# 32 of the 384 dense tokens leave the first expert product; 48 gathers, 52 parked blocks and the gate reads are moved

## The chip, the cores and the metric

The kernel runs on one core of one Trainium2 chip. The core has a matrix engine (TensorE, PE in the profile, with its weight loads as PEld), a vector engine (DVE), a scalar engine (ACT), GpSimd (POOL, which here issues the indirect DMAs), SyncE (SP, which issues the plain DMAs) and 16 DMA engines. The metric is the device time of one execution in microseconds; a run's time is a little longer than the span from its first to its last instruction.

## The reference, cut to what matters

Two layers over 512 tokens of width 1024. Each layer has a mixer (attention in the first, a short convolution in the second) and then a PEER block, and each of the four starts with an RMS norm. The PEER block scores 128 x 128 experts per token through two sets of 128 keys, keeps 16 of them for each of 8 heads (128 per token), and sums the chosen experts' rows:

```
q  = (xc @ w_query) ...                       # per head and half
sv, si = top_k(q . keys, 16)                  # for both halves
cand = sv[0][:, None] + sv[1][None, :]        # 256 candidates
best, pos = top_k(cand, 16); eidx = 128 * i + j
g = softmax(best)
a   = einsum('cd,chkd->chk', xc, w_up[eidx])  # up: one dot product per chosen expert
act = gelu(a) * g
out = einsum('chk,chkd->cd', act, w_down[eidx])
```

Inputs and output are float32; w_up and w_down have 16384 rows of 1024 floats (4 KB) per layer.

## The kernel before, in words

Tokens are in four chunks of 128. In a PEER block the last chunk (c3) is handled **sparsely**: for each of its 128 expert slots, one indirect DMA on POOL's queue fetches 128 rows of w_up (one for each token, 512 KB), and DVE multiplies them with the normed tokens `hn` and sums (L477); later the same for w_down, multiplied by the activation and added to `accg` (L486). These are 256 gathers per layer, through a ring of 4 row buffers.

The other three chunks (TD = 384 tokens) are handled **densely**, for all 16384 experts, in 128 blocks of 128 experts. For each block an *up* (`dense_up`, matmuls at L127) loads 512 KB of transposed w_up, splits it into a high and a low part (ACT L105, DVE L106), and runs 24 matmuls of 128 x 128 by 384 columns (8 pieces of 3 products: high-high, high-low, low-high); ACT applies Gelu to the result `ab` (L499). A *down* (`dense_down`) multiplies `ab` by the gate matrix on DVE (`w`, L520), splits `w`, loads and splits 512 KB of w_down, and runs 18 matmuls of 512 columns into six accumulators that stay in PSUM (L536). Each tensor is kept as a high and a low float32r part.

The gate matrix (weight of each expert for each dense token) is built on the chip in the **retrieval** stage: DVE picks the top 16 (`select`, in the order of chunks 3, 0, 1, 2); then for each four tokens (a *quad*, 96 per layer) DVE and ACT build two sets of one-hot vectors `ob` and `oa`, PE multiplies them (L457), and ACT copies the result to `stage` (L458), which goes to DRAM as `gd` in 12 pieces of 2 MB. While DVE and ACT do this, PE runs ups: the first NPRE = 52 blocks are computed there, and their `ab` is written to DRAM (`ad`): these blocks are *parked*. How many up pieces go between two steps is set by estimated costs: each step yields an estimate for DVE and PE, and pieces (0.49 each) follow while the sum for PE is below PRE_RATE = 1.4 times the sum for DVE.

Then comes the **dense stage**: 128 downs, with the 76 fresh ups between them (AHEAD = 4 blocks ahead) and the 256 gathers spread over the blocks (a parked block counts 1, a fresh one 2; LATE = 0.97 ends them a little early). The gate matrix is read back in groups of 4 blocks (`gt`, 768 KB, two buffers), a parked `ab` in pairs (`at`). Groups of fresh and of parked blocks alternate so that both kinds are used up together. SP, POOL, DVE, ACT and PE each run their instructions in a fixed order, which a planner chose by simulating the program's timeline; `issue_after` ties a gather to its block's `w`.

Each norm (`norm_t`) computes a factor per token, writes it into a diagonal matrix `dg` (L168), and transposes and scales the tokens in one float32 product of `h` with `dg` (L174), 32 products per norm; each shows as two instructions. The gains and the split into high and low follow at L178 and L179.

Of the kernel before, what the change touches and what calls it, by code (L numbers as in the profile page):

```python
# [12 lines left out]
F32 = mybir.dt.float32  # L13
# [10 lines left out]
P = 128  # L24
# [26 lines left out]
NPRE = 52  # L51
PRE_RATE = 1.4
OB = 12
ACTN = 2
# [10 lines left out]
def encoder(ctx: ExitStack, tc: tile.TileContext, x, g_mix, g_ffn, g_ffn_row, g_fin_row, bias,  # L65
# [93 lines left out]
    def norm_t(gain, name, order=range(NCH)):  # L159


        xh = acts.tile([P, KC, S], F32R, name=f"xh{name}", tag="xh")
        xl = acts.tile([P, KC, S], F32R, name=f"xl{name}", tag="xl")
        dg = {}
        for c in order:
            r = rstd_of(c)
            dg[c] = small.tile([P, P], F32, name="dg", bufs=4)
            nc.vector.tensor_scalar(dg[c], ident, r, None, op0=ALU.mult)  # L168
        for k0 in range(0, KC, 4):
            ps = [ps_acc(f"ps_t{k}") for k in range(4)]  # L170
# [5 lines left out]
            for k in range(4):  # L176
                kc = k0 + k
                nc.scalar.activation(xh[:, kc], ps[k], AF.Copy, scale=gain[:, kc:kc + 1])  # L178
                nc.vector.scalar_tensor_tensor(xl[:, kc], ps[k], gain[:, kc:kc + 1], xh[:, kc].bitcast(F32),  # L179
                                               op0=ALU.mult, op1=ALU.subtract)  # L180
        return xh, xl
# [22 lines left out]
    def attention(l):  # L204
        xh, xl = norm_t(gm[:, l], f"m{l}", (3, 0, 1, 2) if l else range(NCH))
# [137 lines left out]
    def short_conv(l):  # L343
        xh, xl = norm_t(gm[:, l], f"m{l}", (3, 0, 1, 2) if l else range(NCH))
# [29 lines left out]
    ad = dram.tile([NPRE // 2, P, 2, TD], F32, name="ad")  # L374

    def peer(l):
        xh, xl = norm_t(gf[:, l], f"f{l}")
        with ExitStack() as st:
# [6 lines left out]
            r3 = rstd_of(c3)  # L385
            nc.vector.scalar_tensor_tensor(hn, h[:, c3], r3, hn, op0=ALU.mult, op1=ALU.mult)
# [24 lines left out]
            g3 = pp.tile([P, P], F32, name="g3")  # L411

            pr = p2

            def retrieval():

                for c in (3, 0, 1, 2):
                    it = select(sv[:, c], si[:, c], pr, cand)
                    while True:
                        try:  # L420
                            yield next(it), 0.0
                        except StopIteration as e:
                            gg, ii, jj = e.value
                            break
                    if c == c3:
                        nc.vector.scalar_tensor_tensor(eid, ii, float(NK), jj, op0=ALU.mult, op1=ALU.add)
                        if l:
                            nc.vector.tensor_scalar(eid, eid, float(l * NK * NK), None, op0=ALU.add)
                        nc.vector.tensor_copy(eidx, eid)
                        nc.vector.tensor_copy(g3, gg)  # L430
                    else:
                        ps = ps_acc("ps_g")
                        for n, t in enumerate((gg, ii, jj)):
                            nc.tensor.transpose(ps[:, n * P:(n + 1) * P], t, ident)
                        for n, t in enumerate((gT, iT, jT)):
                            nc.vector.tensor_copy(t[:, c * P:(c + 1) * P], ps[:, n * P:(n + 1) * P])
# [27 lines left out]
            ab = {}  # L464
            ag = pp.tile([P, P], F32, name="ag")
# [8 lines left out]
            def gather_up(k, t):  # L474
                fetch(up, k, t)
                o = acts.tile([P, D], BF16, name="sq", tag="sq")
                nc.vector.scalar_tensor_tensor(o, t, 1.0, hn, op0=ALU.mult, op1=ALU.mult,  # L477
                                               accum_out=ag[:, k:k + 1])
                if k % 4 == 3:
                    s = ag[:, k - 3:k + 1]  # L480
                    nc.scalar.activation(s, s, AF.Gelu)
                    nc.vector.tensor_tensor(s, s, g3[:, k - 3:k + 1], op=ALU.mult)

            def gather_down(k, t):
                fetch(down, k, t)
                nc.vector.scalar_tensor_tensor(accg, t, ag[:, k:k + 1], accg, op0=ALU.mult, op1=ALU.add)  # L486
# [7 lines left out]

            def dense_up(b):
                for ps in up_pieces(up_t[l, b], xh, xl, TD):
                    yield
                a = pp.tile([P, TD], F32, name="ab", tag="ab", bufs=AHEAD + 2)
# [9 lines left out]
            def dense_down(n, b):  # L508
                if b % 4 == 0:
                    gt = p2.tile([P, TD // GT, 4, GT], F32, name="gt")  # L510
                    nc.sync.dma_start(gt.rearrange("p g i c -> p g (i c)"),
                                      gd[:, :, b:b + 4].rearrange("g j i c -> j g (i c)"))
                    first.append(gt)
                if b < NPRE and b % 2 == 0:
                    at = p2.tile([P, 2, TD], F32, name="at")
                    nc.sync.dma_start(at, ad[b // 2])
                    ab[b], ab[b + 1] = at[:, 0], at[:, 1]
# [3 lines left out]
                                        ab.pop(b).rearrange("p (g c) -> p g c", c=GT), gt[:, :, b % 4], op=ALU.mult)  # L521
# [34 lines left out]

            fresh = list(range(NPRE // 4, NK // 4))
            kept = list(range(NPRE // 4))
            order = []
            for n, q in enumerate(fresh):  # L560
                order.append(q)
                while len(kept) and (NPRE // 4 - len(kept)) * len(fresh) <= n * (NPRE // 4):
                    order.append(kept.pop(0))
            order += kept
            blocks = [4 * q + i for q in order for i in range(4)]
            ng = done = 0
            rows = [p2.tile([P, D], F32, name=f"row{n}", bufs=1) for n in range(RING)]
            nup = NPRE
            for n, b in enumerate(blocks):
# [7 lines left out]
                while ng < len(gathers) and ng * (2 * NK - NPRE) * LATE < done * len(gathers):  # L577
                    fn, k = gathers[ng]
                    with tc.issue_after(mark):
                        fn(k, rows[ng % RING])  # L580
# [168 lines left out]
```

## Time and profile before

| | |
|---|---|
| median of 3 runs | 3028.08 us (3024.51 to 3029.07) |
| profiled execution, its own time | 3023.92 us |
| its span, first to last instruction | 3022.1 us |
| granted TensorE clock, mean | 0.997 |
| PE busy | 2985.9 us (99%) |
| DVE busy | 2337.9 us (77%) |
| ACT busy | 1362.3 us (45%) |
| POOL busy | 658.6 us (22%) |
| DMA moved | 747.96 MB, mean 247 GB/s |

Busy times are of each engine alone; they overlap. A PE that is busy need not be at its best pace, since matmuls are pipelined: the pace is read from the length of a run of matmuls in the chain of waits. The retrieval stages lie at about 400 to 715 us and 1850 to 2170 us, the dense stages at about 730 to 1555 us and 2185 to 3010 us.

### The profile page before, as it was taken

To read this page: it belongs to the slowest core of one execution; us is meant where nothing else is said; L and a number is where in the kernel's file an instruction comes from. 1 tells how busy PE (TensorE), PEld (TensorE's weight loads), DVE (VectorE), ACT (ScalarE), POOL (GpSimd) and SP (SyncE) were. 2 spreads that over 40 slices of the span, in tenths; PEclk is the share of its full clock that TensorE was granted. 3 is DMA by queue.
4 is the path that set the end of the run, shared out by engine and by line. 5 is a ranking of instruction groups with operands and counts; after the bars stand their busy time and mean duration, and the time that the engine had idled before them with its cause. 6 is when DMAs were issued, how large, how long until landed. Compare 5 with 4: busy or idle time off the path is not lost. (4 is left out here: it accounts for less than half of the span.)

```text
span 3022.1 us, 44124 instructions
## 1 busy us (share of the span) xinstructions
PE 2985.9 (99%) x15730; PEld 2677.1 (89%) x15730; DVE 2337.9 (77%) x5115; ACT 1362.3 (45%) x2237; POOL 658.6 (22%) x571
## 2 busy tenths in 40 slices
PE   8999999999999999999999999999999999999998
PEld 7887899999888888888888888999988888888887
DVE  4444899887888888887874489998788888888786
ACT  5444246996333333333342233599733333333333
POOL 0000000001434443443310000000034344444341
PEclk9999999999999999999999999999999999999999
DMA  4222244567999999998942323556699999999995
GB/s 162 95 97 89 87 138 159 220 233 282 340 344 340 337 344 338 333 338 316 340 144 92 108 93 114 171 196 232 239 358 340 334 348 335 340 326 350 324 332 192
DMA packets 297981, 747.96 MB, mean 247 GB/s; under 512 B 23456, under 2 KB 139168, under 8 KB 294688
## 3 DMA queue, kind: packets, MB, share of 16 engines
q1 hardware_dynamic: 224032, 476.67, 45.2%
q0 software_dynamic: 73728, 268.47, 24.0%
q8 instruction: 124, 2.03, 0.3%
q14 instruction: 97, 0.79, 0.1%
HBM read 672.17 MB, written 72.88 MB: 247 GB/s over the span
## 5 line engine op out<-in xcount | busy, mean ns | idle before, releaser
L127 PE MATMUL ps_up<-xhf,wu_l 128*128 128x384 f32 (+1 forms) x2304 | 798.9, 347 | 1.2 <-DVE wu_l L106 1.0
L127 PE MATMUL ps_up<-xhf,wu_h 128*128 128x384 f32 (+1 forms) x2304 | 794.2, 345 | 2.0 <-ACT ab L499 2.0
L127 PE MATMUL ps_up<-xlf,wu_h 128*128 128x384 f32 (+1 forms) x2304 | 792.0, 344 | 0.0
L105 ACT ACTIVATE wu_h<-wu_raw 128x1024 fp32r<-128x1024 f32 x336 | 355.4, 1058 | 710.6 <-PE ps_up L127 430.7
L470 POOL DMA_INDIRECT row<-in_up,eidx x256 | 322.4, 1260 | 1312.9 <-DMA wu_raw<-in_up_t 881.6
L536 PE MATMUL acc<-wd_h,w_l 128*128 128x512 f32 x1536 | 603.7, 393 | 0.1
L536 PE MATMUL acc<-wd_l,w_h 128*128 128x512 f32 x1536 | 599.0, 390 | 0.0
L105 ACT ACTIVATE wd_h<-wd_raw 128x1024 fp32r<-128x1024 f32 x256 | 271.6, 1061 | 702.0 <-issue 619.3
L106 DVE TENSOR_TENSOR wu_l<-wu_raw,wu_h 128x1024 fp32r<-128x1024 f32 x336 | 410.0, 1220 | 176.4 <-ACT wu_h L105 176.1
L536 PE MATMUL acc<-wd_h,w_h 128*128 128x512 f32 x1536 | 514.9, 392 | 0.0
L106 DVE TENSOR_TENSOR wd_l<-wd_raw,wd_h 128x1024 fp32r<-128x1024 f32 x256 | 313.3, 1224 | 235.5 <-ACT wd_h L105 234.9
L127 PEld LDWEIGHTS ps_up<-xhf,wu_h 128*128 128x128 f32 x2304 | 433.3, 188 | 21.1 <-ACT ab L499 3.3
L127 PEld LDWEIGHTS ps_up<-xlf,wu_h 128*128 128x128 f32 x2304 | 433.1, 188 | 17.5
L127 PEld LDWEIGHTS ps_up<-xhf,wu_l 128*128 128x128 f32 x2304 | 433.1, 188 | 17.2 <-DVE wu_l L106 3.7
L470 POOL DMA_INDIRECT row<-in_down,eidx x256 | 330.4, 1291 | 511.7 <-DVE sq L477 464.6
L536 PEld LDWEIGHTS acc<-wd_l,w_h 128*128 128x128 f32 x1536 | 288.4, 188 | 61.7
L486 DVE SCALAR_TENSOR_TENSOR accg<-row,ag,accg 128x1024 f32<-128x1024 f32 x256 | 327.4, 1279 | 16.1 <-DMA row<-in_down,eidx 15.5
L536 PEld LDWEIGHTS acc<-wd_h,w_l 128*128 128x128 f32 x1536 | 288.6, 188 | 55.0 <-DVE w_l L106 0.9
L536 PEld LDWEIGHTS acc<-wd_h,w_h 128*128 128x128 f32 x1536 | 287.2, 188 | 54.8
L477 DVE SCALAR_TENSOR_TENSOR sq<-row,hn 128x1024 bf16<-128x1024 f32 x256 | 312.0, 1219 | 3.9 <-DMA row<-in_up,eidx 2.7
L457 PE MATMUL ps_gb<-ob,oa 128*128 128x128 f32 x1536 | 209.6, 274 | 0.0
L458 ACT ACTIVATE stage<-ps_gb 128x512 f32<-128x512 f32 x192 | 204.6, 1114 | 2.1 <-PE ps_gb L457 1.5
(164 smaller groups left out, 3325.8 us busy)
## 6 DMA issues: line engine op xcount, KB each, us to landing
wd_raw<-in_down SPq DMA_DIRECT2D x256, 512.0 KB, 5.8
wu_raw<-in_up_t SPq DMA_DIRECT2D x256, 512.0 KB, 4.9
gd<-stage SPq DMA_DIRECT2D x24, 2048.0 KB, 7.4
gt<-gd SPq DMA_DIRECT2D x64, 768.0 KB, 9.2
ad<-ab SPq DMA_DIRECT2D x104, 192.0 KB, 2.1
at<-ad SPq DMA_DIRECT2D x52, 384.0 KB, 8.0
wu_raw<-in_w_query SPq DMA_DIRECT2D x32, 512.0 KB, 3.5
wu_raw<-in_w_qkv SPq DMA_DIRECT2D x24, 512.0 KB, 3.5
```

The costliest lines, as they stand in the source:

```text
L105: nc.scalar.activation(hi, raw, AF.Copy)
L106: nc.vector.tensor_tensor(lo, raw, hi.bitcast(F32), op=ALU.subtract)
L127: nc.tensor.matmul(ps[:, :n], a[:, c], b[:, kc, :n], start=k == 0, stop=k == 3 * KC - 1)
L457: nc.tensor.matmul(ps[:, n * NK:(n + 1) * NK], a, b4[:, n], start=True, stop=True)
L458: nc.scalar.activation(stage[:, :, 4 * q:4 * q + 4].rearrange("p i t -> p t i"), ps.rearrange("p (t i) -> p t i", t=4), AF.Copy)
L470: nc.gpsimd.indirect_dma_start(out=t, out_offset=None, in_=table, in_offset=bass.IndirectOffsetOnAxis(ap=eidx[:, k:k + 1], axis=0))
L477: nc.vector.scalar_tensor_tensor(o, t, 1.0, hn, op0=ALU.mult, op1=ALU.mult, accum_out=ag[:, k:k + 1])
L486: nc.vector.scalar_tensor_tensor(accg, t, ag[:, k:k + 1], accg, op0=ALU.mult, op1=ALU.add)
L536: nc.tensor.matmul(acc[c, half], aa[:, cs], ww[:, hs], start=new and i == 0, stop=n == NK - 1 and ww is held[-1][-1])
```

## The change

The last 32 tokens of the third chunk (tokens 352 to 383, a *unit*, UN = 1, UT = 32) no longer take part in the ups: an up has TU = 352 columns. Their up products come from gathers: the 128 partitions hold 32 tokens x 4 groups of slots, so 32 indirect DMAs fetch all 32 x 128 rows, and 32 DVE products with `hu` (the normed tokens, copied to all four groups) give the dots; Gelu, the gate weights and a transpose bring them into `gT`, so that the gate matrix holds activation times weight for these tokens. In `ab` and `at` their columns are set to 1.0 once, and downs are as before, for 384 tokens. The chunks are selected in the order 2, 3, 0, 1. After the unit's 32 gathers the first 48 of the sparse gathers follow, in the retrieval stage too, one step after each `select` step or quad. 104 blocks are parked instead of 52, the gate matrix is read in groups of 8 blocks (1.5 MB), and PRE_RATE is 1.56. In the norms, DVE scales the tokens (`hs`, 1024 columns per chunk) and PE transposes them against the identity; the factors are reused in the PEER block instead of computed again for chunk 3.

```diff
-NPRE = 52
-PRE_RATE = 1.4
+NPRE = 104
+UN = 1
+UT = 32
+TU = TD - UN * UT
+GB = 8
+PRE_RATE = 1.56
+EARLY = 48
 def norm_t(gain, name, order=range(NCH)):
-            dg[c] = small.tile([P, P], F32, name="dg", bufs=4)
-            nc.vector.tensor_scalar(dg[c], ident, r, None, op0=ALU.mult)
+                hs[c] = sp.tile([P, D], F32, name=f"hs{c}")
+                nc.vector.tensor_scalar(hs[c], h[:, c], r, None, op0=ALU.mult)
...
-                    nc.tensor.matmul(ps[k][:, c * P:(c + 1) * P], h[:, c, kc * P:(kc + 1) * P], dg[c],
-                                     start=True, stop=True)
+                        nc.tensor.transpose(ps[k][:, c * P:(c + 1) * P], hs[c][:, kc * P:(kc + 1) * P], ident)
 def peer(l):
-            r3 = rstd_of(c3)
-            nc.vector.scalar_tensor_tensor(hn, h[:, c3], r3, hn, op0=ALU.mult, op1=ALU.mult)
+            nc.vector.scalar_tensor_tensor(hn, h[:, c3], rs[c3], hn, op0=ALU.mult, op1=ALU.mult)
+                t = wpool.tile([P, D], F32, name="hu", tag="wd_h", bufs=2)
+                nc.sync.dma_start(t[q], g_ffn_row[l].to_broadcast([UT, D]))
+                nc.vector.scalar_tensor_tensor(t[q], h[q, cu], rs[cu][q], t[q], op0=ALU.mult, op1=ALU.mult)
+                        nc.scalar.activation(t[g * UT:(g + 1) * UT], t[q], AF.Copy)
...
+            def unit_steps():
+                at = [(u, k) for u in range(UN) for k in range(UT)]
+                for n in range(len(at) + 2):
+                    if n < len(at):
+                        u, k = at[n]
+                        t = wpool.tile([P, D], F32, name="urow", tag="wd_r", bufs=RAW)
+                        nc.gpsimd.indirect_dma_start(
+                            out=t, out_offset=None, in_=up,
+                            in_offset=bass.IndirectOffsetOnAxis(ap=xu[:, u, k:k + 1], axis=0))
+                        urows.append(t)
+                    if n >= 2:
+                        u, k = at[n - 2]
+                        o = acts.tile([P, D], BF16, name="sq", tag="sq")
+                        nc.vector.scalar_tensor_tensor(o, urows.pop(0), 1.0, hu[u][1], op0=ALU.mult, op1=ALU.mult,
+                                                       accum_out=au[:, u, k:k + 1])
+                    yield
 def retrieval():
-                for c in (3, 0, 1, 2):
+                for c in (cu, c3, 0, 1):
...
                             yield next(it), 0.0
+                            for _ in itertools.islice(units, 1):
+                                yield 1.3, 0.0
...
+                        if c == cu:
+                            unit_lists(gg, ii, jj)
+                            units = itertools.chain(unit_steps(), early_steps())
                 for t0 in range(0, TD, GT):
+                    if t0 == TU:
+                        for _ in units:
+                            yield 1.3, 0.0
+                        unit_values()
...
                         yield 1.35, 0.9
+                        for _ in itertools.islice(units, 1):
+                            yield 1.3, 0.0
+            def early_steps():
+                uses = []
+                for n in range(EARLY + 2):
+                    if n < EARLY:
+                        fn, k = gathers[n]
+                        uses.append(fn(k, wpool.tile([P, D], F32, name="erow", tag="wd_r", bufs=RAW)))
+                    if n >= 2:
+                        uses.pop(0)()
+                    yield
 def dense_up(b):
-                for ps in up_pieces(up_t[l, b], xh, xl, TD):
+                for ps in up_pieces(up_t[l, b], xh, xl, TU):
...
-                nc.scalar.activation(a, ps[:, :TD], AF.Gelu)
+                nc.scalar.activation(a[:, :TU], ps[:, :TU], AF.Gelu)
                 if b < NPRE:
-                    nc.sync.dma_start(ad[b // 2, :, b % 2], a)
+                    nc.sync.dma_start(ad[b // 2, :, b % 2], a[:, :TU])
 def dense_down(n, b):
-                if b % 4 == 0:
-                    gt = p2.tile([P, TD // GT, 4, GT], F32, name="gt")
+                if b % GB == 0:
+                    gt = p2.tile([P, TD // GT, GB, GT], F32, name="gt")
...
-            fresh = list(range(NPRE // 4, NK // 4))
-            kept = list(range(NPRE // 4))
+            fresh = list(range(NPRE // GB, NK // GB))
+            kept = list(range(NPRE // GB))
...
-                while ng < len(gathers) and ng * (2 * NK - NPRE) * LATE < done * len(gathers):
+                while ng < len(gathers) and (ng - EARLY) * (2 * NK - NPRE) * LATE < done * (len(gathers) - EARLY):
```

## Rows read from the trace of the kernel before

**Rows 1.** The page: engines (busy us, share, instructions), GB/s in 40 slices.
```profile
PE 2985.9 (99%) x15730; PEld 2677.1 (89%) x15730; DVE 2337.9 (77%) x5115; ACT 1362.3 (45%) x2237; POOL 658.6 (22%) x571
...
GB/s 162 95 97 89 87 138 159 220 233 282 340 344 340 337 344 338 333 338 316 340 144 92 108 93 114 171 196 232 239 358 340 334 348 335 340 326 350 324 332 192
```
**Rows 2.** PE's groups by line and shape: count, busy us, mean ns, idle before.
```profile
L127 PE MATMUL ps_up<-xhf,wu_l 128*128 128x384 f32 x2048 | 699.1, 342 | 1.2 <-DVE wu_l L106 1.0
L536 PE MATMUL acc<-wd_h,w_l 128*128 128x512 f32 x1536 | 603.7, 393 | 0.1
...
L174 PE MATMUL ps_t<-dg,h 128*128 128x128 f32 x256 | 37.4, 309 | 19.7 <-DVE dg L168 19.6
...
L280 PE MATMUL ps_pt<-ident,sc 128*128 128x128 f32 x128 | 21.0, 278 | 1.4 <-ACT sc L269 1.2
```
**Rows 3.** Chain of waits in order of time: start us, us, what.
```profile
1618.08 5.49 PE ps_up L127 x24
...
2201.79 4.12 PE acc L536 x18
...
2247.37 4.19 PE ps_up L127 x24
```
**Rows 4.** The chain's stretch at the end of the second retrieval stage.
```profile
2172.32 0.89 PE ps_gb L457 x8
2173.22 16.47 PE ps_up L127 x95
```
**Rows 5.** Stretches: length, busy us (x) of PE, PEld, DVE, ACT, POOL; clock, DMA share, GB/s.
```profile
730.00:763.00 33.00, 33.00 (x163) 29.28 (x163) 27.64 (x41) 12.84 (x21) 12.82 (x13) 1.00 1.05 404
763.00:780.00 17.00, 17.00 (x81) 14.66 (x80) 12.81 (x17) 6.27 (x9) 5.79 (x5) 1.00 1.02 390
...
1850.00:2168.00 318.00, 316.35 (x2078) 313.19 (x2077) 295.29 (x945) 250.34 (x414) 0.00 (x0) 1.00 0.55 196
...
2216.00:2950.00 734.00, 734.00 (x3588) 652.06 (x3587) 600.25 (x781) 260.64 (x382) 303.87 (x237) 1.00 0.94 336
```
**Rows 6.** DMA issues of the page: count, KB each, median us to landing.
```profile
wd_raw<-in_down SPq DMA_DIRECT2D x256, 512.0 KB, 5.8
...
gt<-gd SPq DMA_DIRECT2D x64, 768.0 KB, 9.2
...
at<-ad SPq DMA_DIRECT2D x52, 384.0 KB, 8.0
```
**Rows 7.** DVE's groups by line and shape, columns as in Rows 2.
```profile
L106 DVE TENSOR_TENSOR wu_l<-wu_raw,wu_h 128x1024 fp32r<-128x1024 f32 x336 | 410.0, 1220 | 176.4 <-ACT wu_h L105 176.1
L486 DVE SCALAR_TENSOR_TENSOR accg<-row,ag,accg 128x1024 f32<-128x1024 f32 x256 | 327.4, 1279 | 16.1 <-DMA row<-in_down,eidx 15.5
...
L477 DVE SCALAR_TENSOR_TENSOR sq<-row,hn 128x1024 bf16<-128x1024 f32 x256 | 312.0, 1219 | 3.9 <-DMA row<-in_up,eidx 2.7
L106 DVE TENSOR_TENSOR w_l<-w,w_h 128x384 fp32r<-128x384 f32 x256 | 141.0, 551 | 1.2 <-ACT w_h L105 1.2
...
L168 DVE TENSOR_SCALAR dg<-ident,r 128x128 f32<-128x128 f32 x16 | 4.4, 282 | 0.0
L360 DVE TENSOR_SCALAR cv<-u,wc 128x512 f32<-128x512 f32 x8 | 3.9, 486 | 0.8
```
**Rows 8.** Waits of PE, by total: us, times, longest.
```profile
PE ps_t L174 <- DVE dg L168: 19.6, 4, 8.4
PE ps_up L127 <- ACT ab L499: 2.0, 2, 1.0
```
**Rows 9.** Timeline of the second layer's second norm: start us, us, engine, line.
```profile
1746.16 7.09 PE L174 MATMUL ps_t<-dg,h 128*128 128x128 f32 x48 [4.88 <-DVE dg L168]
...
1751.72 4.16 ACT L178 ACTIVATE xhf<-ps_t,gf 128x512 fp32r<-128x512 f32 x7 [4.04 <-PE ps_t L174]
```
**Rows 10.** DVE's timeline at the start of the second dense stage.
```profile
2186.79 0.60 DVE L520 TENSOR_TENSOR w<-ab,gt 128x384 f32<-128x384 f32 x1 [3.59 <-DMA gt<-gd]
```

More of the change, by code (lines that the diff above doesn't have):

```diff
@@ L163, in norm_t @@
         xl = acts.tile([P, KC, S], F32R, name=f"xl{name}", tag="xl")
[L164 to L171 removed]
+        rs = {}
+        with tc.tile_pool(name="scaled", bufs=1) as sp:
+            hs = {}
+            for c in order:
+                r = rs[c] = rstd_of(c)
+                hs[c] = sp.tile([P, D], F32, name=f"hs{c}")
+                nc.vector.tensor_scalar(hs[c], h[:, c], r, None, op0=ALU.mult)
+            for k0 in range(0, KC, 4):
+                ps = [ps_acc(f"ps_t{k}") for k in range(4)]
+                for c in order:
+                    for k in range(4):
+                        kc = k0 + k
+                        nc.tensor.transpose(ps[k][:, c * P:(c + 1) * P], hs[c][:, kc * P:(kc + 1) * P], ident)
                 for k in range(4):
                     kc = k0 + k
[L174 to L181 removed]
+                    nc.scalar.activation(xh[:, kc], ps[k], AF.Copy, scale=gain[:, kc:kc + 1])
+                    nc.vector.scalar_tensor_tensor(xl[:, kc], ps[k], gain[:, kc:kc + 1], xh[:, kc].bitcast(F32),
+                                                   op0=ALU.mult, op1=ALU.subtract)
+        return xh, xl, rs
     def out_proj(w, yh, yl):
@@ L204, in attention @@
     def attention(l):
-        xh, xl = norm_t(gm[:, l], f"m{l}", (3, 0, 1, 2) if l else range(NCH))
+        xh, xl, _ = norm_t(gm[:, l], f"m{l}", (3, 0, 1, 2) if l else range(NCH))
         with tc.tile_pool(name="attn", bufs=1) as ap, tc.tile_pool(name="attn2", bufs=2) as a2:
@@ new lines, in unit_lists @@
+            def unit_lists(gg, ii, jj):
+                flat_ids(eid, ii, jj)
+                for u, (q, _) in enumerate(hu):
+                    for g in range(P // UT):
+                        ks = slice(g * UT, (g + 1) * UT)
+                        nc.scalar.activation(fu[ks, u], eid[q, ks], AF.Copy)
+                        nc.scalar.activation(gu[ks, u], gg[q, ks], AF.Copy)
+                nc.vector.tensor_copy(xu, fu)
+            def unit_steps():
[14 more added lines that the diff above has]
+                    yield
@@ new lines, in unit_values @@
+            def unit_values():
+                nc.scalar.activation(au, au, AF.Gelu)
+                nc.vector.tensor_tensor(au, au, gu, op=ALU.mult)
+                ps = ps_acc("ps_u")
+                for u in range(UN):
+                    nc.tensor.transpose(ps[:UT, u * P:(u + 1) * P], au[:, u], ident)
+                for u in range(UN):
+                    for g in range(P // UT):
+                        ks = slice(g * UT, (g + 1) * UT)
+                        nc.scalar.activation(gT[ks, TU + u * UT:TU + (u + 1) * UT],
+                                             ps[:UT, u * P + g * UT:u * P + (g + 1) * UT], AF.Copy)
@@ L464, in peer @@
             ab = {}
+            ring = [pp.tile([P, TD], F32, name=f"ab{n}") for n in range(AHEAD + 2)]
+            for t in ring:
+                nc.gpsimd.memset(t[:, TU:], 1.0)
             ag = pp.tile([P, P], F32, name="ag")
@@ L561, in peer @@
                 order.append(q)
-                while len(kept) and (NPRE // 4 - len(kept)) * len(fresh) <= n * (NPRE // 4):
+                while len(kept) and (NPRE // GB - len(kept)) * len(fresh) <= n * (NPRE // GB):
                     order.append(kept.pop(0))
             order += kept
-            blocks = [4 * q + i for q in order for i in range(4)]
-            ng = done = 0
+            blocks = [GB * q + i for q in order for i in range(GB)]
+            parked = [p2.tile([P, 2, TD], F32, name=f"at{n}", bufs=1) for n in range(2)]
+            for t in parked:
+                nc.gpsimd.memset(t[:, :, TU:], 1.0)
+            ng = EARLY
+            done = 0
             rows = [p2.tile([P, D], F32, name=f"row{n}", bufs=1) for n in range(RING)]
```

61 lines of the change are left out of this document (40 added, 21 removed).

## The prediction

> **What bounds the kernel now.** I read the engines' busy shares first. PE is busy 2985.9 of 3022.1 us, DVE 77%, and from the slices the DMA engines move 316 to 358 GB/s through both dense stages and far less elsewhere [rows 1]. Busy does not mean best pace, so next came the chain of waits: 24 products of 512 columns take 5.49 us, 24 of 384 columns 4.19 us, and one down (18 of 512) 4.12 us, stage after stage [rows 3]. PE's waits are small: 19.6 us in the four norms and little else [rows 8]. So the end is set by PE's amount of work. What comes next is read from the dense stage: in 734 us of it PE is never idle, DVE is busy 82%, and DMA has a share of 0.94 at 336 GB/s [rows 5]. An edit that shortens PE's work there brings DMA and DVE nearer to the end by the same amount.
>
> **1. 352 instead of 384 columns in every up.** A column costs (5.49 - 4.19) / (24 x 128) = 0.423 ns [rows 3], so an up loses 24 x 32 x 0.423 = 0.325 us and takes 3.865 us. There are 128 ups in each of two layers (three groups of 2048 products [rows 2]): 256 x 0.325 = **-83 us**. All of it is on the path, PE being the bound. Bounds: if the whole 4.19 us shrank with the columns, 256 x 4.19 / 12 = -89; if the pace were set by something other than columns, 0. Against the latter stand the gate products of 128 columns, 8 instructions in 0.89 us or 0.111 us each [rows 4], well under the 0.175 us of a 384-column product. I take -83.
>
> **2. The norms.** 128 products with `dg` show as 256 instructions and 37.4 us; a transpose in attention takes 21.0 / 128 = 0.164 us against 37.4 / 128 = 0.292 [rows 2], so 128 transposes take 21.0 us. Per norm, the first 16 products are what ACT waits for [rows 9]; they become 16 x 0.128 = 2.0 us shorter, and so do the other 16. Against that, DVE scales 1024 columns instead of writing a 128 x 128 diagonal: (486 - 282) / 384 = 0.53 ns a column [rows 7], so 0.76 us, 0.48 more for each chunk. If only the first chunk's delay counts and both halves gain, a norm gains 3.6 us; if all four delays count (1.9 us) and only the first half gains, 0.1; if DVE's time counts and the transposes gain nothing, it loses 1.9. I take 1.3 for each of four: **-5 us** (-14 to +8). The reused factors, the `hu` product (1.28 us, as `accg` in [rows 7]) and its three ACT copies come beside PE's 16 query blocks; I cost them at nothing.
>
> **3. Retrieval.** PE's sum does not change by parking more: 52 ups per layer move from the dense stage into this one. What has to hold is the cover. In the second layer the stage lasts 318 us with PE at 316.35 and DVE at 295.29 [rows 5]. PE's work becomes 316 - 52 x 0.325 + 52 x 3.865 = 500 us. DVE gets 52 splits of 1.22, 32 unit products of 1.22 and 48 early ones of 1.25 on average [rows 7]: 295 + 63 + 39 + 60 = 457, which is 91% of 500 where it was 93% of 318. ACT, 250 us before [rows 5], gets 52 more high parts and Gelus; they would have to take 4.8 us each to fill its 500. The new waits: a product on DVE waits for its gather, and the one-hot compares queued behind it are what PE's gate products need. It stands two steps behind its gather, and the 84 steps take PE's 500 us less the first chunk (18.6 x 1.56 / 0.49 = 59 up pieces of 0.483, 28 us) and the 48 quads that have no step (2.46 pieces and 0.89 us of gate products [rows 4] each, 2.1): 371 / 84 = 4.4 us a step, 9 us for two; a row-sized load takes 5.8 [rows 6]. On SP 52 more stores of `ab` per layer wait for a Gelu ahead of the next load of w_up; there are three buffers for those. Nearest row: 256 such products waited for their row for 15.5 us in all [rows 7], so 160 would wait some 10 us, mostly beside other PE work. I take **+3 us** (0 to +60; the upper end if the 80 gathers lengthen DVE's queue by 0.9 us each, which brings it past PE by 30 us a layer).
>
> **4. Into the dense stage.** The first `w` waited 3.59 us for `gt` [rows 10] and ran at 2186.79; then PE needs `w` split (0.55 on DVE [rows 7], about as much on ACT, and the hand-overs: some 2.2 from the start of `w`), 2189.0, while its 95 up products lasted to 2189.69 [rows 4]. The margin is 0.7 us. The first `gt` is now 1.5 MB; its second half is 0.79 MB, 2.0 us at 390 GB/s; 95 shorter products cover 1.3 us less. So 2.6 us a layer: **+5 us** (0 to +12). Later `gt`s have two buffers and are asked for a whole group (8 blocks) ahead.
>
> **5. The dense stage.** PE's work there falls from 52 x 4.12 + 76 x 8.31 = 846 to 104 x 4.12 + 24 x 7.985 = 620 us a layer. Bytes, with 512 KB = 0.524 MB [rows 6]: gathers per parked block go from 256 / (204 x 0.97) = 1.29 to 208 / (152 x 0.97) = 1.41. A parked block then moves 2.41 x 0.524 + 0.197 (`gt`) + 0.180 (`at`) = 1.640 MB, a fresh one 4.82 x 0.524 + 0.197 = 2.724. The same sum for the kernel before gives 332 GB/s over the stage, and the trace shows 336 [rows 5]. Afterwards the stage asks for 236 MB in 620 us = 381 GB/s; a parked block, beside 4.12 us of PE, for **398 GB/s** (387 before), a fresh one for 341. And parked blocks no longer come in groups of 4: the order becomes F P F PPPP F PPPPPPPP in groups of 8, so up to 64 in a row, 264 us at the edge of what DMA can do. What can it do? The start of the first dense stage, where gathers catch up, shows 404 GB/s for 33 us and then 390 for 17 [rows 5], 399 on the mean, with PE at full pace. At 399 a parked block takes 4.11 us and nothing is lost; at 395, 4.15, +7 us for 208 blocks; at 390, +18. DVE: `w`, `w_l`, `wd_l` and 1.41 products are 0.55 + 0.55 + 1.22 + 1.41 x 1.29 = 4.14 us; the same sum for the stretch before (731 us scaled to 846) overstates the 600 / 734 that the trace shows by 5%, so 3.9 of 4.12, near, but under. I take **+7 us** (0 to +130).
>
> The Trainium skill speaks against this step: "DMA: Bandwidth & Descriptors", section Specifications, gives about 358 GB/s as the limit of HBM for one core; by it a parked block would take 4.58 us, +96 us, and the time would be about 3040. This trace disagrees with it as long as one core runs alone: 404 GB/s for 33 us [rows 5].
>
> **Sum**, against the profiled execution's own 3023.9 us (span 3022.1 and 1.8 around it; 4 below the median 3028.08): 3023.9 - 83 - 5 + 3 + 5 + 7 = 2951. **I predict 2952 us.**
>
> **Rivals.**
> *A. DMA holds less than its burst when asked for 264 us on end.* For it: the page's slices of the dense stages lie at 316 to 358 GB/s with the engines nearly all busy [rows 1]; share per GB/s was 0.94 / 336 in the long stretch, which read as capacity is 357. Against it: that stretch asked for only 332, and share per GB/s fell to 1.05 / 404 as soon as more was asked [rows 5]. At 375 GB/s a parked block takes 4.38 us, +53 instead of +7: 2997. 20%.
> *B. The same, below the point where the gain is gone.* Without step 5 the gain is 80 us, 0.386 for each of 208 parked blocks: they break even at 4.51 us, which is 364 GB/s. At 350 they take 4.69, +118: 3062, slower than before. PE would idle before the downs, waiting for `wd_l`, and DVE before `sq` and `accg`. 7%.
> *C. Retrieval becomes DVE's.* If rows come late or compares fall behind, the 30 us a layer of step 3: 2951 + 57 = 3008. For it: DVE stood at 93% there [rows 5]; against: its share falls, and so does ACT's. 5%.
> *D. The narrower product does not run faster.* Then 3023.9 + 10 = 3034, slower. Against it [rows 4]. 3%.
> *E. Better:* nothing in steps 3 to 5, a full gain in the norms: 2927. 10%.
>
> **How the numbers follow.** The forecast's own case (2935 to 2975) gets 55%. E lies just under it, A and C just above; from 2925 to 3010 about 85% is held, and beyond it are B, D and the tail of A. A measurement of this kernel tells 0.2% (6 us) from no change. Slower by more than that: B and D, 9%; within it 3%, from cases between A and B; faster 88%.
>
> **What would show it.** Step 1: 24 products of 352 columns in 3.87 us in the chain. Step 2: the first `xh` of a norm about 1.5 us sooner after the last write of `h`, PE's wait before the norms near 20 us in all. Step 3: PE without idle time in retrieval stages of some 500 us, `urow` and `erow` landing before DVE asks. Step 4: the first down within 3 us of the last covered up. Step 5: 18 products in 4.12 us throughout the runs of parked blocks, at 390 GB/s or more; if I am wrong there, PE's chain shows gaps behind `wd_l` or `w_l`, DVE waits for rows, and the rate stands flat below 390. Wrong altogether would be a dense stage well over 640 us a layer.

## The result, and the profile after

The changed kernel takes 3129.78 us (median of 4 runs, 3124.07 to 3139.44) against 3028.57 beside it: **ratio 1.0344, 95% interval 1.0326 to 1.0361, slower by 3.4%**. Forecast were 2952 us and a range of 2925 to 3010. The profiled execution took 3132.64 us with a span of 3130.9.

The page of the changed kernel: engines, granted clock and GB/s in 40 slices, as in [rows 1].
```profile
PE 2938.8 (94%) x15604; PEld 2600.1 (83%) x15604; DVE 2419.9 (77%) x5242; ACT 1370.6 (44%) x2263; POOL 748.0 (24%) x651
...
PEclk9999999999999999999979999999999999999998
...
GB/s 158 95 95 48 98 158 304 260 299 338 285 230 332 330 360 339 347 338 349 357 194 101 98 70 115 250 291 295 357 330 206 342 342 342 352 340 350 336 340 253
```
PE was busy 99% of a span of 3022; now it is busy 94% of one of 3131. Less work, more idle time. The stretches say where (the columns of [rows 5]: length; busy us of PE, PEld, DVE, ACT, POOL; clock, DMA share, GB/s):
```profile
407.00:947.00 540.00, 513.18 (x3358) 505.67 (x3357) 444.72 (x1110) 334.00 (x546) 113.42 (x86) 0.99 0.78 275
947.00:1588.00 641.00, 616.82 (x2782) 514.08 (x2782) 530.67 (x714) 223.57 (x321) 244.53 (x190) 0.99 0.94 342
1588.00:1632.00 44.00, 4.41 (x24) 3.84 (x24) 31.94 (x56) 7.42 (x17) 16.18 (x18) 0.57 0.57 194
2446.00:3097.00 651.00, 619.69 (x2787) 515.80 (x2786) 537.66 (x721) 222.51 (x320) 247.36 (x197) 0.98 0.94 341
```
They are the first retrieval stage, the first dense stage, what follows its last down, and the second dense stage. PE idles 27 us in the first, 24 in the second, 40 in the third and 31 in the fourth. The rate in the dense stages is 342 GB/s, far from the 381 that the prediction said they would ask for. PE's waits (us in total, times, longest; compare [rows 8]):
```profile
PE ps_t L184 <- DVE r L161: 53.3, 3, 39.8
PE acc L635 <- ACT wd_h L113: 52.5, 22, 4.9
PE ps_up L135 <- DVE wu_l L114: 12.0, 15, 2.4
PE ps_up L135 <- ACT ab L598: 10.1, 13, 2.0
...
PE acc L635 <- ACT w_h L113: 5.5, 2, 4.7
```
And the chain that ended last, from the second retrieval stage on, some of its longest pieces (start us, us, what):
```profile
2330.16 7.36 PE ps_up L135 x46
...
2693.47 25.03 PE acc L635 x108
2721.33 14.17 DMA wd_raw<-in_down
2736.63 19.56 PE acc L635 x77
2762.54 13.26 DMA wd_raw<-in_down
2776.93 19.72 PE acc L635 x84
2797.16 14.66 DMA wd_raw<-in_down
```
An up product of 352 columns takes 7.36 / 46 = 0.160 us, 24 of them 3.84 (3.87 foreseen), and 108 products of a down take 25.03, 4.17 for 18. Step 1's pace is there. But in this part the chain leaves PE every 35 to 40 us for a load of w_down that takes 13 to 15 us; [rows 3 to 4] show a chain of PE alone.

For a ledger I cut each trace at the last key product, the first and last down, and the next norm, and subtract PE's work (its products at the paces that the traces show, 0.161 us for 352 columns, 0.229 for 512, and so on; records missing from a trace make this uncertain by some us a stage). What is left is the excess: idle time of PE, and time in which it ran at a lower clock. The ledger is of the one profiled execution, which lies up to 9 us from a kernel's median. **PE's work fell by 97 us, the excess grew by 206**, all in us:

| | kernel before | changed |
|---|---|---|
| PE's work, whole kernel | 2949 | 2852 |
| excess, start to the first keys | 44.5 | 54.2 |
| excess, retrieval, layers 1 and 2 | 3.1, 3.3 | 39.4, 19.5 |
| excess, dense stage, layers 1 and 2 | 1.0, 0.4 | 35.4, 46.1 |
| from the last down to the norm of layer 2 | 0.2 | 40.2 |
| convolution to the second keys | 8.8 | 13.6 |
| end, after the last down | 12.0 | 30.7 |

**How a gap in the dense stage comes about.** SyncE's queue in the timeline of one gap of the first layer (start us, us, engine, line, operation):
```profile
1322.67 0.52 SPq L615 DMA_DIRECT2D at<-ad  x1
1323.24 0.74 SPq L610 DMA_DIRECT2D gt<-gd  x1
1324.08 7.64 SPq L119 DMA_DIRECT2D wd_raw<-in_down  x3
```
then ACT and PE:
```profile
1336.87 0.52 ACT L113 ACTIVATE w_h<-w 128x384 fp32r<-128x384 f32 x1 [3.60 <-PE acc L635]
1339.22 1.06 ACT L113 ACTIVATE wd_h<-wd_raw 128x1024 fp32r<-128x1024 f32 x1 [1.83 <-DMA wd_raw<-in_down]
```
```profile
1335.25 1.54 PE L635 MATMUL acc<-wd_l,w_h 128*128 128x512 f32 x6
1340.33 0.70 PE L635 MATMUL acc<-wd_h,w_h 128*128 128x512 f32 x1 [3.54 <-ACT wd_h L113]
```
The gate read of 1.5 MB is issued at 1323.24, and three loads of w_down behind it, the first at 1324.08, the third at 1331.39. A load's landing is the last of the 16 completion marks that it leaves in the trace. By these the gate read lands at 1337.27 and the three loads at 1339.20, 1341.07 and 1342.38, that is 15.1, 12.7 and 11.0 us after their issue; ACT waits for the first of them (it starts its split at 1339.22), PE for ACT. Of the loads of w_down between 1200 and 1580 us (70 of 83 have all their marks), one lands 6.6 us after issue in the middle and within 12.8 in nine of ten (before: 5.8 and 7.8), and ACT takes it 2.9 us after it has landed (before: 9.5). The **lead**, from issue to use, shrank from 16.3 to 10.6 us on the mean. From 1000 to 1580 us the first load behind a gate read landed 11.4 to 16.3 us after its issue (ten of them); loads issued more than 14 us after a gate read took 5.8 us in the middle and 8.0 at most.

**The tail.** DVE after the last down of the first layer:
```profile
1613.87 1.28 DVE L573 SCALAR_TENSOR_TENSOR accg<-row,ag,accg 128x1024 f32<-128x1024 f32 x1 [0.54 <-DMA row<-in_down,eidx]
1615.46 1.28 DVE L573 SCALAR_TENSOR_TENSOR accg<-row,ag,accg 128x1024 f32<-128x1024 f32 x1 [0.31 <-DMA row<-in_down,eidx]
```
These are two of 22 gather products that stand behind the layer's last `w` in DVE's order (12 in the second layer, none in the kernel before). PE meanwhile waits 39.8 us for the next norm.

### The profile page after: what moved, and what is told of

Same layout as the page of the kernel before. It is cut to its first block, busy times and chain, and to the rows that moved or that the text cites. A ratio compares the mean times of both kernels' runs of the same rounds, so it can differ in the third digit from the quotient of the medians.

```text
span 3130.9 us, 44476 instructions
## 1 busy us (share of the span) xinstructions
PE 2938.8 (94%) x15604; PEld 2600.1 (83%) x15604; DVE 2419.9 (77%) x5242; ACT 1370.6 (44%) x2263; POOL 748.0 (24%) x651
## 5 line engine op out<-in xcount | busy, mean ns | idle before, releaser
L135 PE MATMUL ps_up<-xhf,wu_h 128*128 128x352 f32 (+1 forms) x2304 | 772.7, 336 | 17.7 <-ACT ab L598 10.1
L135 PE MATMUL ps_up<-xhf,wu_l 128*128 128x352 f32 (+1 forms) x2304 | 775.4, 337 | 12.1 <-DVE wu_l L114 12.0
L135 PE MATMUL ps_up<-xlf,wu_h 128*128 128x352 f32 (+1 forms) x2304 | 765.7, 332 | 0.0
L635 PE MATMUL acc<-wd_h,w_h 128*128 128x512 f32 x1536 | 523.7, 401 | 58.0 <-ACT wd_h L113 52.5
L635 PE MATMUL acc<-wd_l,w_h 128*128 128x512 f32 x1536 | 502.6, 393 | 0.0
L554 POOL DMA_INDIRECT row<-in_up,eidx x200 | 263.1, 1315 | 434.5 <-DVE accg L573 404.6
L554 POOL DMA_INDIRECT row<-in_down,eidx x216 | 262.0, 1213 | 398.2 <-DVE sq L563 370.6
L113 ACT ACTIVATE w_h<-w 128x384 fp32r<-128x384 f32 x256 | 132.9, 519 | 390.7 <-PE acc L635 329.0
L573 DVE SCALAR_TENSOR_TENSOR accg<-row,ag,accg 128x1024 f32<-128x1024 f32 x216 | 276.2, 1279 | 12.8 <-DMA row<-in_down,eidx 11.8
L563 DVE SCALAR_TENSOR_TENSOR sq<-row,hn 128x1024 bf16<-128x1024 f32 x200 | 243.7, 1218 | 5.2 <-DMA row<-in_up,eidx 4.7
```

The costliest lines, as they stand in the source:

```text
L113: nc.scalar.activation(hi, raw, AF.Copy)
L135: nc.tensor.matmul(ps[:, :n], a[:, c], b[:, kc, :n], start=k == 0, stop=k == 3 * KC - 1)
L554: nc.gpsimd.indirect_dma_start(out=t, out_offset=None, in_=table, in_offset=bass.IndirectOffsetOnAxis(ap=eidx[:, k:k + 1], axis=0))
L573: return lambda: nc.vector.scalar_tensor_tensor(accg, t, ag[:, k:k + 1], accg, op0=ALU.mult, op1=ALU.add)
L635: nc.tensor.matmul(acc[c, half], aa[:, cs], ww[:, hs], start=new and i == 0, stop=n == NK - 1 and ww is held[-1][-1])
```

## The experiments

The excess of each kernel by the ledger, layers 1 and 2, in us; "tails" is what follows the last downs beyond the 12 us that the kernel before has at its end:

| kernel | median us, ratio | retrieval | dense | tails |
|---|---|---|---|---|
| gt4 | 3095.41, 1.0233 | 25, 21 | 27, 25 | 34, 26 |
| ring6 | 3138.79, 1.0377 | 26, 20 | 68, 75 | 0, 0 |
| ring6gt4 | 3073.38, 1.0162 | 29, 21 | 42, 41 | 0, 0 |
| e0r6 | 3148.97, 1.0408 | 31, 32 | 76, 73 | 0, 0 |
| e0nounit | 3117.56, 1.0300 | 11, 11 | 77, 81 | 0, 0 |
| v104e96r6 | 3090.61, 1.0215 | 70, 67 | 10, 9 | 0, 0 |
| v80e32r6 | 3039.07, 1.0044 | 25, 21 | 26, 28 | 0, 0 |
| v80e32r8raw4 | 3017.03, 0.9973 | 14, 20 | 28, 18 | 0, 0 |
| raw4r6 | 3025.21, 0.9999 | 16, 21 | 33, 16 | 0, 1 |
| raw4r6gt4 | 3010.00, 0.9951 | 15, 16 | 32, 6 | 4, 0 |
| r6gtact | 3078.48, 1.0172 | 35, 31 | 42, 43 | 0, 0 |

Ratios are to runs of the kernel before on the same chip. The kernels `norms` and `cols` are edits of the kernel before.

**gt4: the gate matrix read in fours again, order of blocks in eights.** (4 runs; 95% interval of the ratio 1.0216 to 1.0250, and so on below)
```diff
-                if b % GB == 0:
-                    gt = p2.tile([P, TD // GT, GB, GT], F32, name="gt")
+                if b % GR == 0:                     # GR = 4
+                    gt = p2.tile([P, TD // GT, GR, GT], F32, name="gt")
...
```


> The changed kernel, but the gate matrix is read back in fours (768 KB) instead of eights (1.5 MB); the order of the blocks stays in groups of eight, 104 parked. Theory Q (queue): the 1.5 MB read holds SP's queue, the loads of w_down behind it land 9 to 11 us after their issue instead of 5, and PE waits once per group, which with the lowered clock makes the dense stages 36 and 46 us longer than PE's work of 604. Then the dense stages fall from 640 and 651 to about 605 to 620 each, and the time from 3130 to about 3070 (gathers left after the last down stay, 18 and 16 in DVE's order instead of 22 and 12). Rival D (rate): the DMA engines give no more than some 345 GB/s in this mix, however the bytes are cut. Then the dense stages stay within 10 us of 640 and 651, and the time within 20 us of 3130.

A third of the loss is gone, less than the theory of the long reads asked and more than that of a flat rate. The dense stages took 352 and 349 GB/s instead of 342 and 341, and nine of ten loads landed within 10.7 us instead of 12.8. PE's waits for the split of w_down, over the whole kernel:
```profile
PE acc L636 <- ACT wd_h L114: 44.0, 29, 1.7
```
The changed kernel has 52.5 us in 22 such waits, of up to 4.9 us, and loses some 20 us of its dense stages to a lower clock after them; gt4 has a granted clock of 1.00 in both dense stages. So of the 29 us that its dense excess is smaller, some 20 are the clock. The length of the read matters; it is not all.

**ring6: six row buffers for the gathers.** (4 runs; 1.0360 to 1.0394)
```diff
-RING = 4
+RING = 6
```


> The changed kernel with 6 row buffers for the sparse gathers instead of 4, nothing else. In DVE's fixed order no gather product is left after the last w of a layer (22 and 12 in the changed kernel). Theory T (tail): the gathers left over cost 40 us between the layers and 18 at the end, because the order was planned with a ring of 4 that could not keep up; then the norm of the second layer starts within 3 us of the last down, the end within 13 us of it, and the time falls by 45 to 58 us to about 3075 to 3085, with dense stages not over 10 us longer each. Rival D (rate flat at some 345 GB/s): the same bytes then have to come within the dense stages, which get longer by what the tails lose, and the time stays within 15 us of 3130.

The tails went, as expected: no gather product is left behind the last `w`. The gain did not come. PE's waits in this kernel:
```profile
PE acc L635 <- ACT wd_h L113: 98.6, 33, 8.5
```
Their total is nearly twice that of the changed kernel. The gathers moved back into the dense stages, and these became longer by as much as the tails had been. So the tail is no cause of its own: it and the dense excess are one loss in two places. **ring6gt4**, both edits, shows what the reads alone bring once tails are out of it (4 runs; 1.0145 to 1.0179): -65 us against ring6.


> Both edits on the changed kernel: gate matrix read in fours, 6 row buffers (no gather left after the last w). In the run with 6 buffers alone the tails went but the dense stages grew to 673 and 679 us; in the run with reads in fours alone they fell to 632 and 634 with tails of 34 and 26 us. Theory Q (the long read in SP's queue is what stalls PE, gathers can be served): dense stages 610 to 630, no tails, time about 3045 to 3065. Rival D (the DMA engines give about 340 to 352 GB/s in this mix and no more): the stage's 228 MB take 650 to 670 us, time 3095 to 3115.

**norms: the kernel before with the new norms alone.** (10 runs; 0.9972 to 0.9991)
```diff
-            dg[c] = small.tile([P, P], F32, name="dg", bufs=4)
-            nc.vector.tensor_scalar(dg[c], ident, r, None, op0=ALU.mult)
+                hs[c] = sp.tile([P, D], F32, name=f"hs{c}")
+                nc.vector.tensor_scalar(hs[c], h[:, c], r, None, op0=ALU.mult)
...
```


> The kernel before with the new norms alone (tokens scaled on DVE, transposed on PE, factors reused). Step 2 of the prediction says -5 us (-14 to +8): 3023. From the stages of the changed kernel, where the four norms and what follows them took about as long as before, I now expect -1: 3027.

3020.43 us, 6 us faster (-5 predicted; the -1 expected just before the run missed). PE's transposes in it, against the `dg` product of [rows 2]:
```profile
L176 PE MATMUL ps_t<-ident,hs 128*128 128x128 f32 x128 | 26.1, 367 | 23.8 <-DVE r L153 9.1 <-DVE v L151 5.7 <-issue 5.4
```
128 instructions instead of 256. Step 2 held in size; PE's work fell by 14 us, so more than half of that was given back.

**cols: the kernel before with ups of 352 columns and nothing in place of the rest.** It leaves out the up products of 32 tokens, whose columns hold 1.0. (4 runs; 0.9872 to 0.9905)
```diff
-                for ps in up_pieces(up_t[l, b], xh, xl, TD):
+                for ps in up_pieces(up_t[l, b], xh, xl, TU):
...
```


> The kernel before with 352 columns in the ups and nothing in their place: the up products of the last 32 dense tokens are left out (their ab is 1.0). It measures step 1 by itself. By step 1 alone, 256 x 0.325 = 83 us less: 2945. If the dense stage is already near what gathers and loads allow, it gives part of it back: DVE's order leaves 8 and 4 gather products after the last w (none before), some 3 us each, so 2960 to 2985. Rival: the narrower products are no faster: 3028.

2992.62 us: -34 where step 1 alone says -83, and a little above the 2960 to 2985 that I expected if part came back. PE's work fell by 82 us. The dense stages did shrink by 30.4 and 28.1 us, but the retrieval stages became 1.7 and 2.9 us longer instead of 11 shorter, and 22 us of tails appeared. The first retrieval stage in it:
```profile
410.00:738.00 328.00, 314.12 (x2177) 311.20 (x2177) 292.46 (x890) 254.89 (x426) 3.91 (x4) 0.99 0.59 209
```
PE is busy 314 us of a stage of 328, so it no longer sets the length. So even without anything in place of the 32 tokens more than half of step 1 is given back; that DVE, with the same 292 us of work, sets the length is read from the row and was not tested by itself.

**e0r6: ring6gt4 without the 48 early gathers** (2 runs; 1.0387 to 1.0429) and **e0nounit: the same without the unit's 32 gathers and products** (2 runs; 1.0280 to 1.0321). The second leaves out the dots of 32 tokens; its other steps stay.
```diff
-EARLY = 48
+EARLY = 0
```


> As the last, but no early gathers (48 more per layer in the dense stage, 25 MB). Theory D: the dense stage follows the bytes, 253 MB at 345 to 350 GB/s = 720 to 735 us each against PE's 604; theory Q: under 650. For the retrieval stage, theory R says that gather products in DVE's order cost the 39 and 20 us by which that stage is longer than PE's work: without 48 of 80 they fall to 10 or less each. Rival: the unit alone or the selects do it, and they stay.

> The run without early gathers (6 row buffers, reads in fours), and now also without the unit's 32 gathers and their products: they are left out, the dots are 0. The steps and the pace of the ups stay. Theory R2: what makes the retrieval stages 31 and 32 us longer than PE's 496 is DVE waiting in its fixed order for the unit's rows; then they fall to 5 to 12 us over PE's work, and the time from 3149 by some 45 us. Rival: it is the up loads, the parked stores or the order of selects and quads around twice as many ups; then they stay over 25. The dense stages stay near 684 and 682.

e0r6 shows what rate can be had, though neither theory's length came (684 and 682 us). Its second dense stage:
```profile
2440.00:3120.00 680.00, 627.85 (x2831) 523.47 (x2830) 606.95 (x820) 227.19 (x335) 365.05 (x250) 0.97 0.98 368
```
368 GB/s for 680 us, where the changed kernel moved 341: that one was not at a ceiling of 341. e0r6's own 73 to 76 us of excess a layer may well be rate: its stage moves 250 MB, which beside PE's 609 us of work asks for 411 GB/s. And 48 gathers fewer in the retrieval stages did not lower their excess. e0nounit took 20 us a layer out of it (the medians differ by 31 us, 45 expected). The same 100 us of the first retrieval stage in e0nounit and in the changed kernel:
```profile
500.00:600.00 100.00, 98.98 (x659) 98.16 (x658) 72.77 (x161) 66.74 (x107) 0.00 (x0) 1.00 0.57 194
```
```profile
500.00:600.00 100.00, 92.24 (x592) 89.79 (x590) 95.67 (x239) 57.73 (x84) 28.84 (x24) 1.00 0.85 291
...
700.00:800.00 100.00, 95.66 (x639) 94.10 (x638) 87.25 (x162) 67.76 (x119) 37.39 (x23) 0.98 0.90 324
```
The unit's products fall where DVE is busiest already: it is at 96% there, and PE idles 8 us of 100. Over the stage's 540 us DVE stands at 82%: a mean hides it. e0nounit leaves out gathers and products together, so it does not tell DVE's added work from its waits for the unit's rows (8.1 us in the first layer).

**v104e96r6, v80e32r6 and v80e32r8raw4: other splits**, with gate reads and order in fours (2, 4 and 8 runs; 1.0195 to 1.0236, 1.0027 to 1.0061, 0.9962 to 0.9984).
```diff
-EARLY = 48
+EARLY = 96          # v104e96r6: GB = 4, RING = 6, PRE_RATE = 1.30
-NPRE = 104
+NPRE = 80           # v80: EARLY = 32, GB = 4, RING = 6 or 8, PRE_RATE = 1.36; raw4 as below
```


> The changed kernel with 96 early gathers instead of 48, reads in fours and blocks in groups of four, 6 row buffers, rate 1.30. It moves 25 MB per layer from the dense stage to retrieval: 211 MB in 604 us is 349 GB/s. Theory D: the dense stages now end with PE, 604 to 620 us, no tails; retrieval gets 48 more products of 1.25 us on DVE, 444 + 60 = 504 us against PE's 500, and takes 550 to 580. Time 3030 to 3090. If the dense stages stay over 635, something other than the bytes holds them.

> The changed kernel balanced by the ledger: 80 blocks parked, 32 early gathers, reads and groups in fours, 6 row buffers, rate 1.36. Dense stage: PE 80 x 4.12 + 48 x 7.985 less the 4 ups ahead = 697 us, 249 MB, 350 to 357 GB/s. Retrieval: DVE about 395, PE about 408. Theory D: dense 700 to 715, retrieval 415 to 435, no tails: 2970 to 3005, faster than before. If retrieval or dense lose as much as in the changed kernel (20 to 40 us each), 3010 to 3070.

> The balanced version (80 parked, 32 early, fours) with 8 row buffers and 4 raw buffers. It stood at 3039 with dense stages 26 and 28 us and retrieval 25 and 21 us over PE's work. If depth is what lacks, both fall to about 10: 2970 to 2990. If the engines' rate is, the dense stages stay over 20 longer: 3020 to 3040.

With 96 early gathers the dense stages are down to 10 and 9 us of excess, and the retrieval stages up to 70 and 67: the load is moved, not removed. 80 parked blocks leave a dense stage with more PE work for its bytes, and 34 us less in all than 104 with the same three load buffers, six row buffers and reads in fours (v80e32r6 against ring6gt4: 3039 and 3073). A fourth load buffer and eight row buffers take another 22 us from it (v80e32r8raw4), and its excess falls, but not to the 10 us a stage that I hoped for.

**raw4r6: ring6 with four load buffers instead of three.** w_up has a set of such buffers, w_down and the rows of the unit and the early gathers share another; a product stands three steps behind its gather, for the fourth row. (10 runs; 0.9989 to 1.0008)
```diff
-RAW = 3
+RAW = 4
...
-                    if n >= 2:
+                    if n >= LAG:        # LAG = 3
```


> The changed kernel (reads in eights, 104 parked, 48 early) with 6 row buffers and 4 buffers instead of 3 for the raw loads of w_up and w_down and for the unit's and early rows (products three steps behind). Theory Q in its second form: PE waits for the split of w_down because its load, 9 to 11 us behind a gate read, has only three buffers (12.4 us of PE) of lead; with four (16.5 us) the dense stages fall from 673 and 679 to 640 or less. Theory D in its second form (the more the gathers ask for, the longer every load takes, and a deeper lead only shifts the wait to the gathers): they stay over 660. Retrieval: if rows that land late are the cause, the stage falls by 10 us or more from 526 and 520.

-114 us against ring6, by one more 512 KB in flight for each of two kinds of load, with the same bytes and gate reads as long. (The third step acts in the retrieval stages alone, and these gave 9 of it.) The dense excess falls from 68 and 75 us to 33 and 16, and PE's waits for the split of w_down from 98.6 us to
```profile
PE acc L636 <- ACT wd_h L114: 11.4, 9, 2.4
```
Between 1200 and 1580 us loads land even later than in ring6 (8.6 us after issue in the middle and within 15.6 in nine of ten, against 6.7 and 14.6), but ACT takes them 6.1 us after that in the middle instead of 2.9: the mean lead is 14.9 us instead of 11.2. **raw4r6gt4** adds the gate reads in fours (4 runs; 0.9934 to 0.9967), **3010.0 us: the best full kernel of this study, 15 us faster than the kernel before.**

> The changed kernel with six row buffers, four load buffers (products three steps behind their gathers) and the gate matrix read in fours. Theory L (loads have too short a lead; a long gate read uses it up, and either a deeper buffer or a shorter read gives it back): the dense stages' excess over PE's work, 33 and 16 us with four load buffers and reads of 1.5 MB, falls to about 10 each; retrieval stays at 16 and 21 us; about 2988 us. Rival S (depth alone was the cause and what is left of the excess is supply: the stage asks for 381 GB/s): no more than with four load buffers alone, 3015 to 3030 us.

PE's largest wait in raw4r6gt4, and its first dense stage's first 55 us:
```profile
PE acc L637 <- ACT wd_h L115: 27.3, 17, 1.6
```
```profile
925.00:980.00 55.00, 55.00 (x294) 50.08 (x294) 47.83 (x59) 20.84 (x31) 24.03 (x21) 1.00 1.04 406
```
In this stage no load is late any more: between 1200 and 1540 us each lies ready at least 3.3 us before ACT takes it. What is left there, 15 waits of 1.6 us of PE, is by the timeline a matter of order: ACT waits for PE to release a buffer before it splits the next load, and PE then for ACT. Of the 37 us expected from the shorter reads 15 came: the second layer's excess went from 16 to 6 us, the first's stayed at 32.

**r6gtact: ring6 with the gate reads issued from ACT's queue.** (4 runs; 1.0155 to 1.0189)
```diff
-                    nc.sync.dma_start(gt.rearrange("p g i c -> p g (i c)"),
+                    nc.scalar.dma_start(gt.rearrange("p g i c -> p g (i c)"),
```


> The changed kernel with six row buffers, and the 1.5 MB gate reads issued from ACT's queue instead of SP's; sizes, buffers and order as in the kernel with six row buffers (3138.8 us, dense excess 68 and 75 us). Theory L1 (the w_down loads are late because they stand behind the gate read in one queue): the loads land about 5 us after issue also behind a gate read, the dense excess falls to 30 us or less each, about 3055 us. Theory L2 (they are late because the read's packets share the 16 DMA engines, whatever the queue): loads behind a read still land after 9 us and more, and the time stays within 15 us of 3139.

Between the two theories: the time falls by 60 us, and the excess in the dense stages by 58 of ring6's 143. PE's waits and the read (count, KB, median us to landing):
```profile
PE acc L635 <- ACT wd_h L113: 62.7, 40, 3.5
PE acc L635 <- issue: 19.1, 2, 9.7
```
```profile
gt<-gd ACTq DMA_DIRECT2D x32, 1536.0 KB, 23.9
```
The longest wait for a split fell from 8.5 to 3.5 us, and the read itself now takes 23.9 us where it took 13.6 in ring6. That has a price at the start of each dense stage: the first gate matrix lands 22.6 and 21.5 us after its issue, and PE stands still for 9.7 and 9.4 us (the second line; 3.5 and 0.4 in ring6), which the ledger counts with retrieval. Standing behind the read in one queue made the long gaps: in the first dense stage (1000 to 1580 us) loads issued while a gate read was under way took 12.5 us in the middle in ring6 and 8.8 here. Moving at the same time as the read remains: the other loads took 6.3 us here, and with a mean lead of 9.6 us PE waits more often, and shorter.

## Why the prediction was wrong, point by point

**1. 352 columns, -83: held as work, not as time.** PE's work fell by 97 us, 14 of it transposes, 83 the ups. But "All of it is on the path, PE being the bound" did not hold even for this step alone: in cols 34 us of time came of it, since the retrieval stages did not get shorter and tails appeared.

**2. Norms, -5: held,** -6 alone (-3 to -8 by the interval).

**3. Retrieval, +3: measured +52** (59 us of excess against 6; 5.5 of it is step 4's pause). I weighed DVE's share over the whole stage and found 91%. The unit's gathers and products come where DVE has the least room (93 to 96% between 430 and 600 us); e0nounit shows 20 us a layer for them, and 11 a layer that stay without them. The rest is not explained: gt4, ring6 and ring6gt4, whose retrieval stages have the same instructions, show 25 to 29 us in the first layer where the changed kernel has 39. Rival C (+57 for DVE as the bound) has this size and, for those 170 us, the mechanism; it had 5%.

**4. Into the dense stage, +5: held.** DVE waited 9.3 and 5.1 us for the first `gt` of the layers, and PE paused 4.7 and 0.8. The step's last sentence, "Later `gt`s have two buffers and are asked for a whole group (8 blocks) ahead", is where the error begins. It is true of the gate reads. I did not ask what a read twice as long does to the loads queued behind it.

**5. The dense stage, +7: the step that failed.** Measured are +80 in the stages, and +59 in the tails that the prediction did not have; the two are one loss, as ring6 shows. I took the stage's need as bytes over time against a rate, "At 399 a parked block takes 4.11 us and nothing is lost". Rate was to be had: 368 GB/s over a whole stage in e0r6, 368 too in the second dense stage of raw4r6gt4 with an excess of 6 us, 406 for 55 us. What was lacking is lead. Three load buffers are worth three blocks of time, less some 3 us for the splits that free them: between 1200 and 1580 us, where blocks took 6.2 us on the mean, a load had 16.3 us from issue to use, and where they take 4.5 it has 10.6. The parked runs that I took as 64 blocks "at the edge of what DMA can do" were at the edge of what a load's latency allows. By depth alone 114 us come back (raw4r6 against ring6), by shorter reads alone 65 (ring6gt4), by both 129.

**Rival B** named the sign that came, PE idle before the downs, waiting for the split of `wd`, and its time (3062) is the nearest. But it made them of a rate under 364 GB/s, and bytes do not order the losses: with some 222 to 230 MB in each dense stage, ring6 loses 68 and 75 us, ring6gt4 42 and 41, raw4r6 33 and 16, raw4r6gt4 32 and 6, and the rate rises from 331 to 368 GB/s as the waits go. The dense stages with their tails came to +139, just over the upper bound of +130 that step 5 had, and which the range left out.

The Trainium skill's limit of about 358 GB/s for one core ("DMA: Bandwidth & Descriptors", section Specifications) would have given the right sign by a wrong reason: the runs, with one core at work, disagree with it as a ceiling: 368 GB/s for 680 us in e0r6.

**Not settled:** some 10 us of excess before the first keys and 5 before the second, of which the new norms alone show 5 each; the first layer's 32 us in raw4r6gt4, read from its waits and not tested; what the 11 us of retrieval in e0nounit are, against 3 before; and what sets the length of the retrieval stages in cols.

## What to carry to other kernels

When a stage gets shorter, its loads' lead shrinks with it: count buffers in time, buffers times the new interval, less the time for which a use holds its buffer, and hold that against the slowest landing, the one behind the longest transfer in its queue, and not against the median or the bytes per second. A share of busy time over a stage must be looked at in slices before work is added to it. A tail and a stall can be one loss in two places: take away the tail first, and see whether the time goes.

## What the runs showed of the hardware

A single load's time depends on what stands ahead of it: in the first dense stage of the changed kernel 512 KB landed in 5.8 us in the middle with no gate read just ahead, and in 11.4 to 16.3 as the first behind a read of 1.5 MB; the read, moved to another queue, took 23.9 us instead of 13.6. And a gap costs more than its length. The granted clock after the gap shown above:
```profile
1340.33:1347.00 6.67, 6.67 (x22) 5.33 (x23) 5.84 (x8) 1.63 (x3) 3.65 (x2) 0.74 0.75 262
1347.00:1360.00 13.00, 13.00 (x58) 10.52 (x57) 11.78 (x17) 4.93 (x8) 6.23 (x5) 1.00 0.93 324
```
After 3.5 us without work PE was granted 0.74 on the mean of the next 6.67 us, about half of them at 1.2 GHz, with products of 512 columns 0.43 us apart instead of 0.23. In the changed kernel's two dense stages such stretches add up to 41 us, some 20 lost. The gaps of up to 1.7 us in gt4 and of 1.6 in raw4r6gt4 were followed by none: their dense stages have a clock of 1.00 throughout.
